# One layer of a pooling and state-space decoder: the sample states' products in one run per half, five raw buffers, exponentials and one split moved

## The chip, the cores and the metric

The kernel runs on one core of one Trainium2 chip. The metric is the device time of one execution in microseconds (us); the lower, the better. The core has several engines, each with its own in-order queue: TensorE (PE, matmuls; its weight loads are shown as PEld), VectorE (DVE), ScalarE (ACT), GpSimd (POOL) and SyncE (SP, which only issues transfers; ACT issues some too). Engines wait for each other by semaphores. Within an engine nothing overtakes: an instruction that waits holds up all that is queued behind it.

## The reference, cut to what matters

There are 1024 prompt rows and 64 sample rows (8 sequences of 8 steps), 1024 channels, one layer, all in fp32. Two branches, causal pooling and a state-space recurrence (SSD), are merged by gates.

```python
shift, scale, gate = split(silu(c) @ w_ada + b_ada)
h = rmsnorm(x, norm_g) * (1 + scale) + shift
u_pool, z_pool, z_ssm, xbc, dt, g = split(h @ w_in)            # 8224 columns
P = (pool_mix(u_pool) * silu(z_pool)) @ w_pool_out
S = gated_rmsnorm(ssd(silu(conv(xbc))) + D * xs, z_ssm) @ w_ssm_out
x = x + gate * ((sigmoid(g_pool) * P + sigmoid(g_ssm) * S) @ w_o)
y = rmsnorm(x, final_g)

# ssd, for each of 4 groups of 8 heads (64 wide, state 128), chunk by chunk
decay = exp(where(mask, acs_i - acs_j, -inf))
att = (C_i . B_j) * decay * dt_j
y   = att @ x  +  C @ (exp(acs) * h)                 # h: the state before the chunk
h   = h * exp(last) + B^T @ (exp(last - acs) * dt * x)
```

For the prompt a chunk has 128 rows and the state starts at zero. For the samples each of the 8 sequences has one chunk of 8 rows and a state that is read from memory (8 x 32 heads x 64 x 128) and written back updated.

## The kernel before

**Products with split operands.** A weight or activation is split into a high part (a copy on ACT, rounded to the matmul's fast fp32r type, tile names `whi`, `Y`, `R`, `S`, `G`) and a low part (the difference, mostly on POOL, `wlo`). Three products, high x high, high x low, low x high, replace one fp32 product. They are lines L609, L610 and L611 in the products with w_in and L360, L361 and L362 in those with w_pool_out and w_ssm_out. Accumulators lie in two pools of PSUM banks: `mm` (3 banks, `PA()`) and `ps` (5 banks, `PB()`).

**The stages.** The head (to about 82 us) makes the modulation (c @ w_ada, L277 among its products) and h with its high and low parts (L315, L327, L330). Then (to about 826 us) w_in is worked off in pairs of 128-column tiles; for each pair seven products of half size replace eight (`strassen`), and the sums on DVE before and after them are L555 (of raw weights) and L620 and L625 (of results). The first part of the pairs feeds convolution and pooling. The last ten "light" pairs (`LAST = 10`, about 600 to 826 us) make gates and z; their function is L721 (on ACT), their results are stored by L723 to memory as `gs` and `gp`. Beside them runs the SSD of the samples, `ssd_samples(g)`, a generator that is moved a step at a time, 18 steps for each of the 4 groups. Then (826 to about 1130 us) come 32 prompt chunks, their work between the products L360 to L362. The tail (from about 1130 us) has the last eight rows of products, `tail_unit(m)`, with row m's split of w_o, and at the end the product with w_o (L2000 to L2002), normalised and stored.

**Raw weights.** `pair_w` loads a pair's weights as two tiles of 512 KB, tag `rawA` with 3 buffers (L541, or L544 in two parts). A buffer is free when its splits and sums (L166 on ACT, L169 on POOL or DVE, L555 on DVE) have read it. The gate weights are loaded by L839 on the same queue, SP.

**The samples' state.** A group's 64 rows are done in two halves of 4 sequences. A half has four parts of two heads each. For a part, PE transposes the four loaded states (L1295, fp32), ACT copies them to SBUF (L1297, tags `hT` and `yt`, in turn), and PE multiplies C by them (L1304): four products of 32 columns, each in its own column tile of the array, out of `cz` (C padded to 32 columns), into a quarter of one bank `po`. An fp32 product is two instructions, so a part has eight. Then comes the update product (L1307) and the update of the state on DVE (L1310), and the state is stored. The products of one part stand behind the next part's transposes.

**Chunks.** A chunk's decays are loaded, `ch_far` masks them on POOL (L1193) and, for all but a group's first chunk, makes `cE`, an exponential on ACT (L1402); `ch_exps` makes eight exponentials on ACT (L1202); `ch_turn` transposes x and B on PE (L118, L1415) and copies B on ACT (L1417); `ch_weigh` weighs x on DVE and copies it on ACT (L1429); `ch_mix` multiplies on DVE (L1439); `ch_lows` makes low parts on DVE (L1444, L1445); `ch_inner` is PE's (L1214).

**What sets the order.** Up to the chunks, the order on each engine is made by a scheduler that simulates the program in time (`schedule_with_timeline_sim`), with the buffers as they come free. `behind(engine)` gives what is issued in it a place not before the engine's last issued instruction. From the chunks on, `in_line` fixes the order as written on all engines, and in the tail on PE, DVE, ACT and POOL.

Of the kernel before, what the change touches and what calls it, by code (L numbers as in the profile page):

```python
# [11 lines left out]
ALU = mybir.AluOpType  # L12
# [34 lines left out]
def tile_pool_ssd_step(  # L47
# [9 lines left out]
    def nm(s):  # L57
        uid[0] += 1
        return f"{s}_{uid[0]}"
# [36 lines left out]
    def PB():  # L96
        return psB.tile([P, 512], F32, tag="ps", name=nm("ps"))
# [104 lines left out]

    def x_square(i, eng):
        xt, n = xr[i]
        sqj = pa.tile([P, D], F32, tag="rawA", name=nm("sqj"), bufs=3)
        if eng is V:
            V.scalar_tensor_tensor(sqj[:n], xt[:n], 1.0, xt[:n], ALU.mult, ALU.mult, accum_out=ss[:n, i:i + 1])
        else:
            act(sqj[:n], xt[:n], AF.Square, accum_out=ss[:n, i:i + 1])
# [70 lines left out]
    def ada_out(part):  # L280
        a, b = PARTS[part]
        n = (b - a) * P // 2
        mr = pa.tile([P, 256], F32, tag="rawA", name=nm("mr"), bufs=3)
        act(mr[:, :n], pm[part][:, :n], AF.Copy)
        return mr

# [246 lines left out]
    def pair_w(c0, c1, pri, early):  # L533
        def run():
            with tc.high_priority(pri):
                raws = []
                for j in range(2):
                    r = pa.tile([P, 4, 2, P], F32, tag="rawA", name=nm("rawA"), bufs=3)
                    rows_ = w_in[0, j * 512:(j + 1) * 512]
                    if c1 == c0 + P:  # L540
                        load(r, rows_[:, c0:c0 + 2 * P].rearrange("(k p) (t c) -> p k t c", p=P, c=P))  # L541
                    else:
                        for t, c in enumerate((c0, c1)):
                            load(r[:, :, t], rows_[:, c:c + P].rearrange("(k p) c -> p k c", p=P))  # L544
                    raws.append(r)
            b11, b12, b21, b22 = raws[0][:, :, 0], raws[0][:, :, 1], raws[1][:, :, 0], raws[1][:, :, 1]
            w = []

            def add(x):
                with tc.high_priority(pri):  # L550
                    w.append(split(x, highs, eng=V if early else None))

            def diff(dst, x, y, op=ALU.subtract, eng=V):
                with tc.high_priority(pri):
                    eng.tensor_tensor(dst, x, y, op)  # L555
# [664 lines left out]
    def spt(shape, tag, bufs, dt=F32):  # L1220
        return sp.tile(list(shape), dt, tag=tag, name=nm(tag), bufs=bufs)

    def ssd_samples(g):
# [36 lines left out]
        for hf in range(2):  # L1260
# [22 lines left out]
            V.memset(cz, 0.0)  # L1283
            V.tensor_copy(cz[:, :, 0:8], Cf[:, 32 * hf:32 * hf + 32].rearrange("p (b i) -> p b i", i=8))
            yield
            po = None
            hts = {}
            for q in range(5):
                if q < 4:
                    j = 4 * hf + q  # L1290
                    if j + H0B - 1 < 8:
                        h0_load(j + H0B - 1)
                    pt = PB()
                    for b in range(4):
                        nc.tensor.transpose(pt[:, b * P:(b + 1) * P], h0s[j][:, b, :], ident)  # L1295
                    hts[q] = spt([P, 512], ("hT", "yt")[q % 2], 1)
                    act(hts[q], pt, AF.Copy)  # L1297
                if q > 0:
                    r = q - 1
                    h0 = h0s.pop(4 * hf + r)  # L1300
                    if po is None:
                        po = PB()
                    for b in range(4):
                        mm(po[32 * b:32 * b + 32, r * P:(r + 1) * P], cz[:, b, :], hts[r][:, b * P:(b + 1) * P],  # L1304
                           start=True, stop=True)
                    pu = PB()
                    mm(pu, xh[:96, r * P:(r + 1) * P], Bb[:96].rearrange("p b n -> p (b n)"), start=True, stop=True)  # L1307
                    for b in range(4):
                        cc_ = 32 * hf + 8 * b + 7
                        V.scalar_tensor_tensor(h0[:, b, :], h0[:, b, :], E2[:, r, cc_:cc_ + 1],  # L1310
                                               pu[:, b * P:(b + 1) * P], ALU.mult, ALU.add)
                    store_(new_ssm_s[0, 4 * hf:4 * hf + 4, 8 * g + 2 * r:8 * g + 2 * r + 2]
                           .rearrange("b h p n -> (h p) b n"), h0)
                if q < 4:
                    yield
            yo = spt([P, 512], "hT", 1)
            act(yo, po, AF.Copy)
            yield
# [277 lines left out]
    def samples_beside():  # L1596
        due[0] += 1
        if due[0] == 7 * LAST - 4:
            with behind(mybir.EngineType.SP):
                next(p_in)  # L1600
        if due[0] == 7 * LAST - 3:
            with behind(mybir.EngineType.SP):
                first_g.append(R())
                load(first_g[0], gp_d[0])
                first_ws[0] = ready(wp_d[0])()
        if due[0] == 7 * LAST - 2:
            next(p_in)
            with behind(mybir.EngineType.SP):
                ch_load(1)
                d_load(1)  # L1610
                first_ws[1] = ready(wp_d[1])()
                ch_load(2)
                d_load(2)
        if due[0] == 7 * LAST - 1:
            with behind(mybir.EngineType.Activation):
                ch_far(0)
                ch_exps(0)
        if due[0] == 7 * LAST:
            with behind(mybir.EngineType.DVE):
# [136 lines left out]
    ENGS = (mybir.EngineType.PE, mybir.EngineType.DVE, mybir.EngineType.Activation, mybir.EngineType.Pool, mybir.EngineType.SP,)  # L1756
    in_line(ENGS, True)
    z_load(0)
    ch_turn(0)
    ch_weigh(0)  # L1760
    ch_far(1)
# [136 lines left out]
    def tail_unit(m):  # L1898
        pf, run_ = S_unit(3, m, m_done)

        def run(w):
            k = m + EARLY
            if k < 8:
                wo_load(k, M((P, D)))
            if 0 < m < 6:
                r_load(m + 2)
            run_(w, 0)
            if m == 0:
                run_(w, 1)
# [12 lines left out]
            if m > 1:  # L1922
                samples[m - 2]()
        return (pf, run)
# [129 lines left out]
```

## Time and profile before

| what | value |
|---|---|
| time, median of 3 runs | 1290.96 us (1286.81 to 1292.78) |
| the profiled execution | 1292.2 us, of which span 1290.4 us |
| mean granted TensorE clock | 0.995 |
| busy: PE, DVE, ACT, POOL | 1255.1, 911.8, 718.4, 675.5 us |
| moved by DMA | 234.9 MB, 182 GB/s |

A row of a timeline gives the start in the span, the duration, the engine, the line, the operation, out<-in, the tiles' sizes, and how many alike were put together; in brackets stand the engine's idle time before it and what ended that. Matmuls overlap: a matmul starts when the one before it has been fed in, not when it has ended, so that steps from start to start are PE's pace. In a list of waits stand microseconds in total, how many there were, and the longest.

### The profile page before, as it was taken

Reading aid. Unit: us, or ns where it says so; the run is one execution under the profiler, and the core shown is the slowest. Engines: PE = TensorE matmul, PEld = TensorE weight load, DVE = VectorE, ACT = ScalarE, POOL = GpSimd, SP = SyncE. Lnnn points to the kernel's source line nnn. Section 1 sums busy time; section 2 is a strip of 40 time slices with the busy share of each in tenths; the row PEclk is TensorE's granted clock in tenths of the full one; section 3 lists DMA queues with packets and bytes.
Section 4 is the critical chain, followed back from the end, with each engine's and each line's share of the span. In section 5 each row is a group of like instructions: output and inputs, shape, how many; then the busy total and the mean of one; then the engine's idle time right before and its main releaser. Section 6 shows DMA issues by size and latency. Waiting matters only on the chain. (4 is left out here: it accounts for less than half of the span.)

```text
span 1290.4 us, 26363 instructions
## 1 busy us (share of the span) xinstructions
PE 1255.1 (97%) x9771; PEld 1176.8 (91%) x9771; DVE 911.8 (71%) x1584; ACT 718.4 (56%) x1685; POOL 675.5 (52%) x555
## 2 busy tenths in 40 slices
PE   7999999999999999999999999999999999999997
PEld 6779999989999999999889999989999999989786
DVE  4686778865979588776667665488667879767533
ACT  4665356465556655554554564686887768522211
POOL 1007658678869777564344443446465656636000
PEclk9999999999999999999999999999999999999999
DMA  9736354465456453444546555889666666575431
GB/s 329 243 116 220 117 164 160 143 198 178 142 164 219 144 184 126 152 154 121 160 134 202 168 155 157 288 289 317 221 197 184 185 215 207 161 270 181 158 105 50
DMA packets 225730, 234.90 MB, mean 182 GB/s; under 512 B 30370, under 2 KB 177010, under 8 KB 225595
## 3 DMA queue, kind: packets, MB, share of 16 engines
q1 hardware_dynamic: 155808, 159.01, 39.6%
q10 hardware_dynamic: 69794, 74.22, 16.8%
q8 instruction: 77, 1.26, 0.4%
q14 instruction: 51, 0.41, 0.1%
HBM read 158.67 MB, written 74.62 MB: 181 GB/s over the span
## 5 line engine op out<-in xcount | busy, mean ns | idle before, releaser
L169 POOL TENSOR_TENSOR wlo<-rawA,whi 128x512 fp32r<-128x512 f32 x120 | 186.8, 1561 | 186.6 <-ACT whi L166 102.0
L169 POOL TENSOR_TENSOR wlo<-raw,whi 128x512 fp32r<-128x512 f32 x92 | 149.4, 1631 | 125.1 <-ACT whi L166 120.7
L360 PE MATMUL mm<-Y,whi 128*128 128x352 f32 (+1 forms) x480 | 160.0, 333 | 2.7 <-DVE G L1890 2.5
L361 PE MATMUL mm<-Y,whi 128*128 128x352 f32 (+1 forms) x480 | 157.8, 329 | 0.4 <-DVE Y L1516 0.4
L362 PE MATMUL mm<-Y,wlo 128*128 128x352 f32 (+1 forms) x480 | 157.3, 328 | 0.0
L611 PE MATMUL mm<-Y,wlo 128*128 128x272 f32 x496 | 143.7, 290 | 4.1 <-POOL wlo L169 3.6
L609 PE MATMUL mm<-Y,whi 128*128 128x272 f32 x496 | 146.4, 295 | 0.3 <-ACT whi L166 0.2
L609 PE MATMUL ps<-Y,whi 128*128 128x272 f32 x496 | 144.4, 291 | 2.2 <-ACT o L809 1.6
L610 PE MATMUL ps<-Y,whi 128*128 128x272 f32 x496 | 143.1, 289 | 0.0
L610 PE MATMUL mm<-Y,whi 128*128 128x272 f32 x496 | 142.8, 288 | 0.0
L611 PE MATMUL ps<-Y,wlo 128*128 128x272 f32 x496 | 142.6, 288 | 0.0
L166 ACT ACTIVATE whi<-rawA 128x512 fp32r<-128x512 f32 x125 | 78.0, 626 | 97.9 <-PE ps L610 43.2
L1057 DVE SCALAR_TENSOR_TENSOR GA<-GA,cvT,GA 128x1112 f32<-128x1112 f32 x72 | 126.4, 1758 | 0.3
L166 ACT ACTIVATE whi<-raw 128x512 fp32r<-128x512 f32 x96 | 58.8, 626 | 90.7 <-DVE raw L555 39.3
L611 PEld LDWEIGHTS mm<-Y,wlo 128*128 128x128 f32 x496 | 93.4, 188 | 6.0 <-POOL wlo L169 4.9
L609 PEld LDWEIGHTS ps<-Y,whi 128*128 128x128 f32 x496 | 93.3, 188 | 3.7 <-ACT o L809 1.8
L360 PEld LDWEIGHTS mm<-Y,whi 128*128 128x128 f32 x480 | 90.6, 189 | 5.5 <-DVE G L1890 3.5
L609 PEld LDWEIGHTS mm<-Y,whi 128*128 128x128 f32 x496 | 93.3, 188 | 2.4 <-ACT whi L166 0.9
L610 PEld LDWEIGHTS mm<-Y,whi 128*128 128x128 f32 x496 | 93.4, 188 | 0.7 <-issue 0.6
L610 PEld LDWEIGHTS ps<-Y,whi 128*128 128x128 f32 x496 | 93.3, 188 | 0.3 <-issue 0.2
L611 PEld LDWEIGHTS ps<-Y,wlo 128*128 128x128 f32 x496 | 93.5, 188 | 0.2 <-issue 0.2
L361 PEld LDWEIGHTS mm<-Y,whi 128*128 128x128 f32 x480 | 90.5, 189 | 2.6 <-DVE Y L1516 0.9
(459 smaller groups left out, 3842.8 us busy)
## 6 DMA issues: line engine op xcount, KB each, us to landing
rawA<-in_w_in SPq DMA_DIRECT2D x46, 512.0 KB
dec<-acs_d SPq DMA_DIRECT2D x32, 512.0 KB
xbc<-GA ACTq DMA_DIRECT2D x24, 512.0 KB
xb<-xbc SPq DMA_DIRECT2D x32, 384.0 KB
rawA<-in_w_in SPq DMA_DIRECT2D x32, 256.0 KB
pw<-in_w_ssm_out ACTq DMA_DIRECT2D x32, 256.0 KB
ws<-ph ACTq DMA_DIRECT2D x32, 256.0 KB
ws<-pw SPq DMA_DIRECT2D x32, 256.0 KB
```

The costliest lines, as they stand in the source:

```text
L166: ins = act(hi[:, :, :ncols], raw[:, :, :ncols], AF.Copy)
L169: (eng or nc.gpsimd).tensor_tensor(lo[:, :, :ncols], raw[:, :, :ncols], hi[:, :, :ncols].bitcast(F32), ALU.subtract)
L360: mm(ps[:, :n], a, rh[k][:, o:o + n], start=(k == 0), stop=False)
L361: mm(ps[:, :n], a, rl[k][:, o:o + n], start=False, stop=False)
L362: mm(ps[:, :n], b, rh[k][:, o:o + n], start=False, stop=(k == nk - 1))
L609: mm(p, hi, ah, start=(k == 0), stop=False)
L610: mm(p, hi, al, start=False, stop=False)
L611: mm(p, lo, ah, start=False, stop=(k == 3))
L1057: V.scalar_tensor_tensor(d[:, :n], rp[:, k:k + n], cvT[:, 24 * k + mc:24 * k + mc + 1], d[:, :n], ALU.mult, ALU.add)
```

## The change

1. In `ssd_samples` the four parts' products with C are issued in one run of 32 instructions at the end of the half, the last part's first (r = 3, 0, 1, 2). Since all four copies are then alive together, they have four tags: `hT`, `yt`, `hU`, `hV`, two more tiles of 2 KB per partition. `po` is taken just before the run. The update products keep their places behind the next part's transposes; the last one stands behind the run. A half has as many steps as before.
2. Tag `rawA` has five buffers, not three, 8 KB more per partition; two other users of the tag say so too (`sqj`, `mr`).
3. `ch_far(0)` is no longer issued behind ACT's last instruction, and `ch_exps(0)` moves from the end of the light pairs to the start of the chunks.
4. In the tail, the split of w_o for row 0 is issued between row 0's first and second third of products, not after the third.

```diff
-        sqj = pa.tile([P, D], F32, tag="rawA", name=nm("sqj"), bufs=3)
+        sqj = pa.tile([P, D], F32, tag="rawA", name=nm("sqj"), bufs=5)
...
-                    r = pa.tile([P, 4, 2, P], F32, tag="rawA", name=nm("rawA"), bufs=3)
+                    r = pa.tile([P, 4, 2, P], F32, tag="rawA", name=nm("rawA"), bufs=5)
...
-            po = None
             hts = {}
-            for q in range(5):
-                if q < 4:
...
-                    hts[q] = spt([P, 512], ("hT", "yt")[q % 2], 1)
-                    act(hts[q], pt, AF.Copy)
+
+            def update(r):
+                h0 = h0s.pop(4 * hf + r)
+                pu = PB()
+                mm(pu, xh[:96, r * P:(r + 1) * P], Bb[:96].rearrange("p b n -> p (b n)"), start=True, stop=True)
...
+            for q in range(4):
+                j = 4 * hf + q
+                if j + H0B - 1 < 8:
+                    h0_load(j + H0B - 1)
+                pt = PB()
+                for b in range(4):
+                    nc.tensor.transpose(pt[:, b * P:(b + 1) * P], h0s[j][:, b, :], ident)
+                hts[q] = spt([P, 512], ("hT", "yt", "hU", "hV")[q], 1)
+                act(hts[q], pt, AF.Copy)
                 if q > 0:
-                    r = q - 1
-                    h0 = h0s.pop(4 * hf + r)
-                    if po is None:
-                        po = PB()
-                    for b in range(4):
-                        mm(po[32 * b:32 * b + 32, r * P:(r + 1) * P], cz[:, b, :], hts[r][:, b * P:(b + 1) * P],
-                           start=True, stop=True)
...
+                    update(q - 1)
+                yield
+            po = PB()
+            for r in (3, 0, 1, 2):
+                for b in range(4):
+                    mm(po[32 * b:32 * b + 32, r * P:(r + 1) * P], cz[:, b, :], hts[r][:, b * P:(b + 1) * P],
+                       start=True, stop=True)
+            update(3)
             yo = spt([P, 512], "hT", 1)
...
         if due[0] == 7 * LAST - 1:
-            with behind(mybir.EngineType.Activation):
-                ch_far(0)
-                ch_exps(0)
+            ch_far(0)
...
     z_load(0)
+    with behind(mybir.EngineType.Activation):
+        ch_exps(0)
     ch_turn(0)
...
             run_(w, 0)
             if m == 0:
+                wo_split(k, w4[0][:, m, :D], w4[1][:, m, :D])
                 run_(w, 1)
                 run_(w, 2)
...
-            if m < 4:
+            if 0 < m < 4:
                 wo_split(k, w4[0][:, m, :D], w4[1][:, m, :D])
-            elif k < 8 and m < 6:
+            elif m and k < 8 and m < 6:
                 wo_split(k, M((P, D), F32R), M((P, D), F32R))
```

On PE, before, in the first half of the samples' first group (row 4344 and on): a part's transposes, the products of the part before it with C, its update product, among weight products.

```order
L609 MATMUL mm_8551<-Y_484,whi_8104 128x272
L610 MATMUL mm_8551<-Y_485,whi_8104 128x272
L1295 MATMUL ps_8378<-ident,h_1359_8175 128x128 x4
L1304 MATMUL ps_8324<-yt_8322,cz_8267 32x128 x4
L1307 MATMUL ps_8389<-dec_8265,dec_8259 128x512
L611 MATMUL mm_8551<-Y_484,wlo_8105 128x272
```

On PE, now, at the end of that half (row 4369 and on); a change of line numbers comes with the diff, the products with C are L1313 now, the update products L1291 and the transposes L1304.

```order
L610 MATMUL ps_8418<-G_757,whi_8033 128x272
L611 MATMUL ps_8418<-G_756,wlo_8034 128x272
L1313 MATMUL ps_8452<-hV_8394,cz_8267 32x128 x4
L1313 MATMUL ps_8452<-hT_8277,cz_8267 32x128 x4
L1313 MATMUL ps_8452<-yt_8322,cz_8267 32x128 x4
L1313 MATMUL ps_8452<-hU_8378,cz_8267 32x128 x4
L1291 MATMUL ps_8469<-dec_8265,dec_8259 128x512
L609 MATMUL ps_8493<-Y_484,whi_8037 128x272
```

The four sets with C, which stood in four places, each between other kinds of products, now follow each other directly, 24 rows behind the last part's transposes.

On ACT, before, at the passage from the light pairs to the chunks (row 1165 and on; an ACT_TABLE_LOAD stands where the next function needs another table):

```order
L721 ACTIVATE u_1851_10958<-u_1851_10958 128x272 x2
L723 DMA gs_147<-u_1851_10958 128x544
L1202 ACT_TABLE_LOAD
L1202 ACTIVATE dec_10994<-dec_10994,acT 128x128 x8
L721 ACT_TABLE_LOAD
L721 ACTIVATE u_1850_10957<-u_1850_10957 128x272 x2
L723 DMA gs_148<-u_1850_10957 128x544
L1417 ACTIVATE bt_11239<-ps_11232 128x128
L1429 ACTIVATE xw_11245<-ps_11231 128x512
L1402 ACT_TABLE_LOAD
L1402 ACTIVATE cE_11248<-dec_11134 128x1024
```

And now (row 1168 and on):

```order
L721 ACTIVATE u_1851_10958<-u_1851_10958 128x272 x2
L723 DMA gs_147<-u_1851_10958 128x544
L721 ACTIVATE u_1850_10957<-u_1850_10957 128x272 x2
L723 DMA gs_148<-u_1850_10957 128x544
L1202 ACT_TABLE_LOAD
L1202 ACTIVATE dec_10994<-dec_10994,acT 128x128 x8
L1417 ACTIVATE bt_11239<-ps_11232 128x128
L1429 ACTIVATE xw_11245<-ps_11231 128x512
L1402 ACTIVATE cE_11248<-dec_11134 128x1024
```

The pair's last function moved ahead of the exponentials, and two of three table loads are gone.

On DVE, before, in the first half of the samples' second group, near 660 us (row 791 and on; L1251 and L1259 to L1280 are the samples' own, the rest sums of pairs):

```order
L625 TENSOR_TENSOR u_1429_8548<-u_1429_8548,ps_8898 128x272
L1251 TENSOR_TENSOR dec_8851<-dec_8851,ps_8874 64x8x64
L620 TENSOR_TENSOR u_1492_8928<-s_1491_8927,mm_9000 128x272
L1259 TENSOR_TENSOR xd_8914<-ps_8959,xd_8914 128x4x64
L620 TENSOR_TENSOR u_1493_8929<-u_1492_8928,mm_9049 128x272
L1270 TENSOR_TENSOR xw_8978<-ps_8971,wd_7450 96x512
L1278 TENSOR_TENSOR bt_8983<-ps_8976,bt_8983 32x128
```

And now:

```order
L625 TENSOR_TENSOR u_1429_8548<-u_1429_8548,ps_8898 128x272
L1251 TENSOR_TENSOR dec_8851<-dec_8851,ps_8874 64x8x64
L1259 TENSOR_TENSOR xd_8914<-ps_8959,xd_8914 128x4x64
L1270 TENSOR_TENSOR xw_8978<-ps_8971,wd_7450 96x512
L620 TENSOR_TENSOR u_1492_8928<-s_1491_8927,mm_9000 128x272
L1278 TENSOR_TENSOR bt_8983<-ps_8976,bt_8983 32x128
L620 TENSOR_TENSOR u_1493_8929<-u_1492_8928,mm_9044 128x272
```

The two samples' sums moved ahead of the pair's first L620. Elsewhere the scheduler moved rows too: on SP, the second pair's raw weight loads stand ahead of the second half of the gate weights' loads; on DVE two sums L555 of that pair moved from row 149 to rows 79 and 83, among the head's last sums for h; on PE the rows 438 to 545 (the second pair's products) are in another order, and the rows from 546 to 4315 stand as before. In the tail, POOL's first L1730 (L1728 now) stands ahead of L1886, not behind it.

More of the change, by code (lines that the diff above doesn't have):

```diff
@@ L282, in ada_out @@
         n = (b - a) * P // 2
-        mr = pa.tile([P, 256], F32, tag="rawA", name=nm("mr"), bufs=3)
+        mr = pa.tile([P, 256], F32, tag="rawA", name=nm("mr"), bufs=5)
         act(mr[:, :n], pm[part][:, :n], AF.Copy)
@@ L1285, in ssd_samples @@
             yield
-            po = None
             hts = {}
-            for q in range(5):
-                if q < 4:
[L1290 to L1293, printed above, removed]
-                    for b in range(4):
-                        nc.tensor.transpose(pt[:, b * P:(b + 1) * P], h0s[j][:, b, :], ident)
-                    hts[q] = spt([P, 512], ("hT", "yt")[q % 2], 1)
-                    act(hts[q], pt, AF.Copy)
-                if q > 0:
-                    r = q - 1
-                    h0 = h0s.pop(4 * hf + r)
-                    if po is None:
-                        po = PB()
-                    for b in range(4):
-                        mm(po[32 * b:32 * b + 32, r * P:(r + 1) * P], cz[:, b, :], hts[r][:, b * P:(b + 1) * P],
-                           start=True, stop=True)
[L1306 to L1315, printed above, removed]
@@ new lines, in update @@
+            def update(r):
[3 more added lines that the diff above has]
+                for b in range(4):
+                    cc_ = 32 * hf + 8 * b + 7
+                    V.scalar_tensor_tensor(h0[:, b, :], h0[:, b, :], E2[:, r, cc_:cc_ + 1],
+                                           pu[:, b * P:(b + 1) * P], ALU.mult, ALU.add)
+                store_(new_ssm_s[0, 4 * hf:4 * hf + 4, 8 * g + 2 * r:8 * g + 2 * r + 2]
+                       .rearrange("b h p n -> (h p) b n"), h0)
@@ L1316, in ssd_samples @@
+            for r in (3, 0, 1, 2):
+                for b in range(4):
+                    mm(po[32 * b:32 * b + 32, r * P:(r + 1) * P], cz[:, b, :], hts[r][:, b * P:(b + 1) * P],
+                       start=True, stop=True)
+            update(3)
             yo = spt([P, 512], "hT", 1)
```

## The prediction

> **What bounds the kernel now.** I read the page's busy times first, then its slices, then the list of what TensorE (PE) waited for.
>
> ```profile
> PE 1255.1 (97%) x9771; PEld 1176.8 (91%) x9771; DVE 911.8 (71%) x1584; ACT 718.4 (56%) x1685; POOL 675.5 (52%) x555
> PE   7999999999999999999999999999999999999997
> ```
>
> PE works 1255.1 of 1290.4 us; no other engine passes 71%. Only the first and the last slice are below 9. So two things can shorten the span: fewer PE microseconds, or fewer PE waits, 35.3 us in all. An engine beside PE matters only where PE waits for it.
>
> ```profile
> PE mm L611 <- POOL wlo L169: 4.7, 8, 1.1
> PE mm L360 <- DVE G L1890: 2.5, 1, 2.5
> PE ps L1295 <- DVE xd L1259: 2.4, 1, 2.4
> PE ps L118 <- DVE btl L1444: 2.1, 1, 2.1
> PE ps L1214 <- DVE dec L1439: 0.6, 1, 0.6
> ```
>
> (us in total, times, longest.) These are the waits that the change can reach. The windows give the stretches between head and tail:
>
> ```profile
> 82.00:600.00 518.00, 510.38 (x3997) 500.35 (x3997) 399.06 (x622) 288.06 (x670) 365.83 (x233) 1.00 0.49 158
> 600.00:826.00 226.00, 221.54 (x1897) 205.39 (x1896) 139.97 (x333) 115.15 (x248) 98.59 (x78) 0.99 0.58 175
> ```
>
> First number after the window: its length, then PE busy. PE is idle 7.6 and 4.5 us there, 12.1 us in 744.
>
> **Column-tiled products, one run of four sets instead of four runs.** The instructions stay the same; only their neighbours change. One set of before, among weight products:
>
> ```profile
> 628.13 0.29 PE L611 MATMUL mm<-Y,wlo 128*128 128x272 f32 x1
> 628.35 0.42 PE L1304 MATMUL ps<-yt,cz 128*32 128x128 f32 x8
> 628.70 0.39 PE L609 MATMUL ps<-Y,whi 128*128 128x272 f32 x1
> 628.93 0.29 PE L610 MATMUL ps<-Y,whi 128*128 128x272 f32 x1
> 629.06 0.29 PE L611 MATMUL ps<-Y,wlo 128*128 128x272 f32 x1
> ```
>
> Starts are what counts, since ends overlap. Undisturbed, a weight product starts 0.13 after the one before it (628.93 to 629.06). From 628.13 to 628.93 there are 0.80 us, with two such steps in it (0.25), so the set costs 0.55: 0.35 from its own start to the next product's, about 0.09 more than usual to get in and about 0.10 more on the first product behind it. With 4 groups, 2 halves and 4 sets that is 32 × 0.55 = 17.6 us. What a longer run costs is shown by the head, where the same shape stands in runs of two lengths, and a copy of a transposed state on ACT:
>
> ```profile
> 26.80 1.52 PE L277 MATMUL ps<-Y,scT 128*32 128x128 f32 x48
> 29.47 0.64 PE L277 MATMUL ps<-Y,scT 128*32 128x128 f32 x16
> 663.67 0.60 ACT L1297 ACTIVATE hT<-ps 128x512 f32<-128x512 f32 x1 [0.16 <-PE ps L1295]
> ```
>
> 32 more instructions take 0.88 us: eight of them, one set, are two rounds of four column tiles, and a further round costs 0.88/8 = 0.11. A run of four sets has eight rounds, six more than one set: 0.55 + 6 × 0.11 = 1.21 us. Eight runs: 9.7 us. Gain 8.0. Lower end: if sets don't close up, each keeps its 0.35, a run is 0.55 + 3 × 0.35 = 1.60, and the gain 4.8. Upper end: if the 0.10 on leaving a run falls away too, 8.8. I take 8.0, since L277's rows have the very shape. What covers the wait for the fourth copy: in each of the eight halves 23 or more PE rows stand between the last state's transposes and the run, 23 × 0.13 = 3 us, against the copy's 0.60. If ACT is over 2 us behind, PE waits there. The last update product and its store come later by a run, 1.2 us, and nobody in the same half waits for them.
>
> **The first exponentials, moved on ACT.**
>
> ```profile
> 826.95 0.44 DVE L625 TENSOR_TENSOR u<-u,ps 128x272 f32<-128x272 f32 x1 [1.07 <-PE ps L611]
> 827.64 1.28 ACT L1202 ACT_TABLE_LOAD   x1 [1.24 <-DMA xb<-xbc]
> 828.93 2.45 ACT L1202 ACTIVATE dec<-dec,acT 128x128 f32<-128x128 f32 x8
> 831.40 1.28 ACT L721 ACT_TABLE_LOAD   x1
> 832.69 0.75 ACT L721 ACTIVATE u<-u 128x272 f32<-128x272 f32 x2
> 833.90 0.28 ACT L1417 ACTIVATE bt<-ps 128x128 fp32r<-128x128 f32 x1 [0.46 <-ACT u L721]
> 834.69 1.28 ACT L1402 ACT_TABLE_LOAD   x1
> 835.98 1.06 ACT L1402 ACTIVATE cE<-dec 128x1024 f32<-128x1024 f32 x1
> 837.11 1.09 POOL L1193 TENSOR_SCALAR_AFFINE_SELECT dec<-dec 128x1024 f32<-128x1024 f32 x1 [12.79 <-ACT cE L1402]
> 834.27 1.22 DVE L1439 TENSOR_TENSOR dec<-dec,ps 128x1024 f32<-128x1024 f32 x1 [3.16 <-issue]
> 841.27 1.22 DVE L1439 TENSOR_TENSOR dec<-dec,ps 128x1024 f32<-128x1024 f32 x1 [2.46 <-ACT ps L1419]
> 835.54 1.09 PE L1214 MATMUL ps<-dec,xd 128*64 128x128 f32 x16 [0.56 <-DVE dec L1439]
> 843.97 0.25 PE L118 MATMUL ps<-identR,xb 128*128 128x128 f32 x1 [2.13 <-DVE btl L1444]
> ```
>
> ACT loads a table three times in seven microseconds, since the last gate function (L721) stands between two groups of exponentials. Now L721 comes first, and the exponentials and cE (L1402) share one load: two loads of 1.28 go. In the new order L721's pair can start when DVE's L625 has summed its operand, 826.95 + 0.44 = 827.4, and ends at 828.15; load and exponentials (1.28 + 2.45) end at 831.9, 2.0 before the 833.90 at which chunk 0's L1417 started. From there to cE were 0.79 and a load; without the load cE ends at 831.9 + 0.8 + 1.06 = 833.8 instead of 837.0. POOL's L1193, next exponentials and L1417 of chunk 1 follow, 3.2 earlier. DVE's first L1439, which waited for the ACT copies, comes 2.0 earlier, more than the 0.56 that PE waited; the second some 3.2 earlier, more than 2.13. Both waits go: 2.7 us, lower end 0.6 (only the first one). Late next is ACT's own pace, a chunk's exponentials and copies, of which L118's wait is the next to return: PE reaches it 0.6 earlier, DVE 3.2 earlier, and 3.2 − 2.1 − 0.6 leaves 0.5 to spare.
>
> ```profile
> 667.50:670.90 3.40, 3.01 (x19) 2.58 (x19) 3.27 (x8) 1.63 (x3) 0.86 (x1) 0.51 0.01 2
> 845.00:848.40 3.40, 3.40 (x20) 3.02 (x20) 3.40 (x8) 2.89 (x10) 2.62 (x4) 0.50 1.08 354
> ```
>
> Behind the 2.13 us wait the granted clock (third from the end) is 0.50 for 3.4 us, and 0.51 behind the 2.4 us wait at 665: half of 3.4 is 1.7 us of work lost each time. I let it go with its wait: another 1.7 (0 to 1.7). Together 4.4.
>
> The Trainium skill, "TensorE: Matmul & The Clock Gate", section "Why this matters for your kernels", warns of PE gaps above about 3 us only, and Part 1 has the clock drop after an idle window of some 3.4 us that runs freely. The trace differs: its gaps are 2.1 and 2.4 us. By that rule the slow stretches would hang on windows and not on these waits, and might stay: 3.4 us less gain (a rival below).
>
> **Five raw weight buffers.** Two buffers more, so SP issues a pair's loads earlier, and the scheduler, which plans with the buffers, puts splits and sums elsewhere: PE rows differ from row 438 to 545 and again in the samples' part.
>
> ```profile
> SPq L541 <- POOL wlo L169: 207.4, 37, 15.6
> 539.19 0.69 DVE L555 TENSOR_TENSOR raw<-rawA,rawA 128x512 f32<-128x512 f32 x1 [6.74 <-DMA rawA<-in_w_in]
> 80.01 0.72 DVE L503 TENSOR_TENSOR Y<-tf,Y 128x544 fp32r<-128x544 f32 x1 [1.52 <-ACT Y L510]
> ```
>
> SP waits 207 us for those buffers, but PE waits for the splits (L611, first list) only 4.7. That is the upper end of the gain; the lower end is a loss, below. I take 1.0, nearer to nothing, since even where DVE stood 6.74 us for a load (539.19) none of PE's eight split waits was over 1.1. In the head two L555 sums (0.69 each) now stand in DVE's queue among the sums of h (L327, L315), before 80 us: 1.4 us, which the idle 1.52 at 80.01 swallows if the loads have landed. If not, DVE stands there and PE waits for h: by the row at 539.19, 6.74 − 1.5 = 5.2 us lost. Loads cost no more bytes; two of them pass gate loads on SP's queue.
>
> The same new plan moves L1259 and L1270 ahead of one L620 on DVE:
>
> ```profile
> 667.07 0.44 DVE L620 TENSOR_TENSOR u<-s,mm 128x272 f32<-128x272 f32 x1 [6.15 <-DMA gp<-u]
> 667.42 0.42 DVE L1259 TENSOR_TENSOR xd<-ps,xd 128x256 f32<-128x256 f32 x1
> 667.89 1.11 PE L1295 MATMUL ps<-ident,h 128*128 128x128 f32 x4 [2.39 <-DVE xd L1259]
> ```
>
> L620 waits 6.15 us for a store to leave its buffer; L1259 behind it holds a PSUM bank that PE's transposes want. With L1259 in front, DVE does it before it stops at L620. PE's 2.4 goes, and the slow clock behind it (1.7): 4.1, lower end 0 if PE then stops at what else L620 holds, its accumulator. I take 4.1.
>
> **Row 0's split of w_o.**
>
> ```profile
> 1147.02 4.76 POOL L1730 TENSOR_TENSOR Y<-m,Y 128x1024 fp32r<-128x1024 f32 x2
> 1149.45 3.42 DVE L1866 TENSOR_TENSOR m<-G,m 128x1024 fp32r<-128x1024 f32 x1
> ```
>
> Two POOL subtractions, 2.4 each, run beside DVE's L1866, which takes 3.42; behind it stands L1890, for which PE waits 2.5 (first list). One subtraction now goes ahead of L1886 into POOL's idle time; the other still meets L1866, as it waits for ACT's half of row 1. Gain between 0 and 2.5; I take 0.5.
>
> **New waits.** A plan in another order has waits of its own. Upper end: as much as the 12.1 us of idle in the two windows above; lower end 0. I take a quarter, 3.0, since most rows there keep their place.
>
> **Sum.** 8.0 + 4.4 + 1.0 + 4.1 + 0.5 − 3.0 = 15.0. The profiled execution took 1292.2 us, 1.2 over the median of the three runs (1290.96); 1292.2 − 15.0 = 1277.2. I give 1277.
>
> **Rivals.**
> 1. Only the run pays. The plan's order gives new waits where it takes old ones, and ACT's chain stays late, waiting for a load (the 1.24 before 827.64). For it: PE idles under 2% between head and tail, so little can be won from waits. Against it: ACT's two loads are seen to go in the new order. 1292.2 − 8.0, and up to 1 us for the first wait at 835: about 1284.
> 2. The slow stretches stay, elsewhere (the rule above): 15.0 − 3.4 = 11.6, about 1280.5. For it: two cases are few to tie a gap to the clock. Against: both stretches stand right behind such a gap, and in the window of 744 us quoted above the clock is 0.99 to 1.00.
> 3. No change that counts: run 4.8, new waits of 3 to 5 eat it: 1288 to 1292. This needs the sets not to close up, against L277's rows.
> 4. Slower: PE waits in each half for the fourth copy (hV), which stands in ACT's queue behind other work. Eight waits of w us; the sum's 15 us are gone at w = 1.9, and past 2 us each would bring 1.7 of slow clock, so w = 2.5 gives 1292.2 − 15 + 8 × 4.2 = 1311. For it: ACT is in order and 115 of 226 us busy there. Against: 3 us of products stand in between, and a copy takes 0.6.
> 5. More: the tail's 2.5 goes as well and new waits stay under 1: about 1272.
>
> **Chances.** Forecast (1274 to 1279) 0.35; rival 2 (1279 to 1282.5) 0.20; rival 1 (1282.5 to 1286) 0.20; rival 5 (under 1274) 0.12; rival 3 0.08; rival 4 0.05. A measurement of this kernel tells about 0.5% from no change, 6.5 us: faster means under 1284.5. The forecast, rivals 2 and 5 and most of rival 1 lie there: 0.35 + 0.20 + 0.12 + 0.13 = 0.80. Within 0.5%: 0.07 of rival 1 and rival 3, 0.15. Slower 0.05. The range leaves out the far end of rival 5, the upper half of rival 3 and rival 4: 1270 to 1286.
>
> **What would show it.** Right: L1313 in eight runs of 32 instructions, about 1.0 us from the first start to the next product's; no ACT_TABLE_LOAD between the L721 near 828 and cE; no PE wait of 2 us near 665 and 843, and 1.00 in the clock there; PE busy near 1243 (8.0 and the slow stretches' 3.4 less). Wrong: a wait of PE for hV, a longer list of PE waits between 82 and 600 us, or DVE standing at its new L555 in the head for a raw weight load, where every microsecond beyond the 1.5 of idle at 80 would be lost.

## The result and the profile after

The changed kernel takes 1273.35 us (median of 6 runs, 1270.23 to 1277.6), the kernel before 1289.32 on the same chip (6 runs, 1286.6 to 1292.78): a ratio of 0.9878, 95% interval 0.9864 to 0.9891, or 16.0 us between the medians. Forecast were 1277 (1270 to 1286) and, against the profiled execution of before, 15.0 us. The profiled execution after takes 1271.29 us with a span of 1269.5, 20.9 less than the span before; so this pair of profiles shows about 5 us more than the medians do, and the runs below were partly made to find out what comes and goes with the execution.

The page after, busy times and PE's slices:

```profile
PE 1242.3 (98%) x9771; PEld 1173.9 (92%) x9771; DVE 900.9 (71%) x1584; ACT 718.0 (57%) x1683; POOL 683.1 (54%) x555
PE   7999999999999999999999999999999999999997
```

PE has the same 9771 instructions and 12.8 us less to do. Two table loads are gone from ACT (1683 instructions for 1685). PE's waits after (us in total, times, longest):

```profile
PE mm L609 <- ACT whi L166: 2.2, 3, 1.1
PE mm L611 <- POOL wlo L169: 2.0, 1, 2.0
PE ps L118 <- DVE btl L1444: 1.4, 1, 1.4
PE mm L609 <- DVE u L620: 1.2, 1, 1.2
PE ps L1291 <- DVE dec L1275: 1.0, 2, 0.6
```

The waits of 2.5 before L360 and of 2.4 before the transposes are gone, the one before L118 fell from 2.1 to 1.4, and three kinds of wait are new or grown. The run of four sets, at the end of the first half:

```profile
616.00 0.29 PE L611 MATMUL ps<-G,wlo 128*128 128x272 f32 x1
616.22 0.42 PE L1313 MATMUL ps<-hV,cz 128*32 128x128 f32 x8
616.46 0.40 PE L1313 MATMUL ps<-hT,cz 128*32 128x128 f32 x8
616.68 0.40 PE L1313 MATMUL ps<-yt,cz 128*32 128x128 f32 x8
616.90 0.40 PE L1313 MATMUL ps<-hU,cz 128*32 128x128 f32 x8
617.23 0.50 PE L1291 MATMUL ps<-dec,dec 96*128 96x512 f32 x1
617.57 0.29 PE L609 MATMUL ps<-Y,whi 128*128 128x272 f32 x1
```

From 616.22 to 617.23 the run takes 1.01 us; a set behind another costs 0.22, two rounds of 0.11, as L277's rows had it. The way in costs 0.22 for 0.13 as before, and the last set needs 0.33 up to L1291, 0.11 more than the others.

Where the time went is best seen by stages. PE's weight products are the same in every kernel, so the starts of the same products (by their count, the first, 600th, 1650th, 3300th, 3900th and last product of the pairs; the 120th and 1000th of those with w_pool_out and w_ssm_out; the last matmul) cut each trace into the same stages, the columns of the table in order. This table is worked out from the traces of all kernels that were run; in "passage", "tail" and others an s marks a stretch of slow clock in that stage.

```
kernel           head  to 160  160-300  300-515  515-590  samples  passage  chunks    tail
before         81.80s   77.60   143.25   215.25    85.19  223.55s  35.45s   230.04  191.58
before again   80.04    78.55   140.53   215.25    85.98  223.91s  35.48s   230.04  191.58
run alone      80.11    78.53   141.53   215.25    85.09  216.94s  33.52    230.04  192.59s
buffers alone  80.09    77.95   138.80   215.25    80.92  224.45s  37.03s   230.04  192.60s
exps alone     79.50    78.56   141.08   215.25    85.13  222.79s  31.92    230.00  193.17s
split alone    79.46    78.44   139.50   215.25    86.39  221.72   35.20s   230.04  190.29
changed        79.64    77.53   138.23   215.25    80.93  218.30s  32.56    230.04  190.29
changed again  79.41    77.44   138.51   215.25    80.90  216.29   32.74    230.00  191.83s
no run         79.14    77.72   138.44   215.25    80.90  224.81s  33.18    230.00  190.24
no buffers     79.86    78.57   142.82   215.25    85.35  215.10   32.11    230.00  190.24
no exps        81.29s   78.04   138.51   215.25    80.91  215.01   38.66s   230.04  190.27
run as 0,1,2,3 81.30s   78.00   138.22   215.25    80.91  218.73s  33.11    230.00  191.79s
four buffers   81.58s   78.03   140.97   215.36    80.89  215.99   34.84s   230.04  190.29
six buffers    81.22s   78.03   139.01   215.25    80.91  219.44s  31.19    230.04  190.25
```

### The profile page after: what moved, and what is told of

Read it like the earlier page. It is cut to its first block, busy times and chain, and to the rows that moved or that the text cites. A ratio compares the mean times of both kernels' runs of the same rounds, so it can differ in the third digit from the quotient of the medians.

```text
span 1269.5 us, 26341 instructions
## 1 busy us (share of the span) xinstructions
PE 1242.3 (98%) x9771; PEld 1173.9 (92%) x9771; DVE 900.9 (71%) x1584; ACT 718.0 (57%) x1683; POOL 683.1 (54%) x555
## 5 line engine op out<-in xcount | busy, mean ns | idle before, releaser
L169 POOL TENSOR_TENSOR wlo<-rawA,whi 128x512 fp32r<-128x512 f32 x120 | 189.0, 1580 | 170.5 <-ACT whi L166 95.8
L169 POOL TENSOR_TENSOR wlo<-raw,whi 128x512 fp32r<-128x512 f32 x92 | 155.1, 1693 | 122.2 <-ACT whi L166 119.3
L360 PE MATMUL mm<-Y,whi 128*128 128x352 f32 (+1 forms) x480 | 159.8, 333 | 0.7
L609 PE MATMUL mm<-Y,whi 128*128 128x272 f32 x496 | 146.3, 295 | 2.2 <-ACT whi L166 2.2
L611 PE MATMUL mm<-Y,wlo 128*128 128x272 f32 x496 | 143.5, 290 | 2.5 <-POOL wlo L169 2.0
L609 PE MATMUL ps<-Y,whi 128*128 128x272 f32 x496 | 143.8, 290 | 0.0
L611 PE MATMUL ps<-Y,wlo 128*128 128x272 f32 x496 | 142.5, 287 | 0.0
L609 PEld LDWEIGHTS mm<-Y,whi 128*128 128x128 f32 x496 | 93.5, 189 | 4.2 <-ACT whi L166 2.8
L611 PEld LDWEIGHTS mm<-Y,wlo 128*128 128x128 f32 x496 | 93.5, 189 | 2.9 <-POOL wlo L169 2.2
L360 PEld LDWEIGHTS mm<-Y,whi 128*128 128x128 f32 x480 | 90.3, 188 | 4.2 <-DVE G L1890 2.4
L609 PEld LDWEIGHTS ps<-Y,whi 128*128 128x128 f32 x496 | 93.3, 188 | 0.2
L611 PEld LDWEIGHTS ps<-Y,wlo 128*128 128x128 f32 x496 | 93.4, 188 | 0.0
```

The lines of the kernel that those rows point to most:

```text
L169: (eng or nc.gpsimd).tensor_tensor(lo[:, :, :ncols], raw[:, :, :ncols], hi[:, :, :ncols].bitcast(F32), ALU.subtract)
L360: mm(ps[:, :n], a, rh[k][:, o:o + n], start=(k == 0), stop=False)
L609: mm(p, hi, ah, start=(k == 0), stop=False)
L611: mm(p, lo, ah, start=False, stop=(k == 3))
```

## The experiments

Where a kernel changes one part, the rest is as in the kernel it is made from; none leaves work out.

**The run alone, the buffers alone, the exponentials alone, the split alone.** Each is the kernel before with one numbered part of the change, so its diff is that part's.

> The kernel before with the run of four sets alone (buffers, exponentials and the split of w_o as before). If a longer run saves what the sum said, 0.55 us becomes 0.22 to 0.24 for three of four sets: 8.0 us less PE time, median near 1281 against 1289, and each run of L1313 about 1.0 us from its first start to the next product. If the places that the scheduler gives to the rest of the samples' work cost as much again (the rival: new waits), the PE time is still 8 less, but the span falls by less than 5 and waits of PE between 600 and 826 us grow by the difference.

> The kernel before with five raw weight buffers alone. In the two traces PE lost 5.0 us less between 195 and 300 us and 4.3 less between 515 and 590 us, in places where the order on PE is the same row by row. First theory: the buffers did that (loads issued earlier, splits never late): median 7 to 10 us under the kernel before, and those waits for the splits (L611 for L169) are gone here too. Rival, the predicted 1.0: such waits come and go from one execution to the next, and the median falls by 0 to 2 us.

> The kernel before with the exponentials moved alone. Predicted 4.4 (2.7 of waits, 1.7 of slow clock); the changed kernel's trace shows 2.9 for this place, since 1.4 of the wait before L118 stays. If the slow clock hangs on the wait, 2.9 to 4.4 less; if it moves elsewhere, 1.0 to 1.5 less. Two table loads fewer on ACT in either case.

> The kernel before with row 0's split of w_o moved alone. Predicted 0.5; the changed kernel's trace shows the 2.5 us wait before L360 gone and 1.3 left of that at the end. So 0.5 to 1.5 less, which the median can hardly show; the rows show whether DVE's L1866 takes 1.2 instead of 3.4 us.

Against 1288.95 us (29 runs of before on that chip):

| kernel | median, runs | ratio, 95% interval |
|---|---|---|
| run alone | 1284.0, 8 | 0.9956 (0.9942 to 0.9969) |
| buffers alone | 1286.43, 10 | 0.9979 (0.9967 to 0.9991) |
| exponentials alone | 1287.86, 10 | 0.9981 (0.9967 to 0.9994) |
| split alone | 1287.22, 10 | 0.9983 (0.9966 to 1.0) |

*The run*: 5.0 us for 8.0 of PE time saved (its page has PE busy for 1245.4 us, 9.7 less than before; 1.7 of that goes with one slow stretch less). In the column "samples" the six executions without the run need 221.7 to 224.8 us and the eight with it 215.0 to 219.4, 6.6 less between the means. The wait near 665 us is gone, and another stands some 30 us earlier:

```profile
PE ps L1291 <- DVE dec L1275: 3.2, 3, 2.6
PE mm L611 <- POOL wlo L169: 1.1, 1, 1.1
```

These are PE's waits between 590 and 828 us in the run alone. The update product waits for the low part of the samples' inputs; the row shows the place.

```profile
638.09 0.50 PE L1291 MATMUL ps<-dec,dec 96*128 96x512 f32 x1 [2.59 <-DVE dec L1275]
```

Behind it the clock is slow for 3.4 us. So the rival of new waits was half right: 8.0 and the old wait were saved, and 5.0 remained.

*The buffers*: the first theory is right about the stages and wrong about the time. From 515 to 590 us every kernel with four buffers or more needs 80.9 and every one with three 85.1 to 86.4, 4.6 more between the means; from 160 to 300 us the kernels with three need 139.5 to 143.3, with five 138.2 to 138.8. Windows of before, cut at round times that cover most of the two stages, and of after, cut at the stages' ends, show PE's idle time vanish (length, PE busy):

```profile
160.00:300.00 140.00, 136.30 (x1059) 132.75 (x1058) 108.60 (x169) 78.72 (x191) 103.33 (x62) 1.00 0.53 172
515.00:590.00 75.00, 72.13 (x563) 70.17 (x562) 57.89 (x95) 37.37 (x82) 45.03 (x40) 1.00 0.43 144
```

```profile
157.20:295.40 138.20, 138.20 (x1085) 135.75 (x1084) 110.80 (x172) 80.13 (x194) 107.71 (x65) 1.00 0.56 179
510.65:591.60 80.95, 80.95 (x642) 79.36 (x641) 65.06 (x104) 41.37 (x84) 51.36 (x44) 1.00 0.42 135
```

PE waits for nothing at all there after the change. Of this, the median of the buffers alone shows 2.5, and its profile names a part of what is missing. The passage takes 1.6 more than before, though both have one slow stretch in it: ACT's copy L1429 waits for the store of the last gate result, which it doesn't in the kernel before, and PE waits 1.5 for L1429.

```profile
824.10 0.33 ACTq L723 DMA_DIRECT2D gs<-u  x1
824.47 0.28 ACT L1417 ACTIVATE bt<-ps 128x128 fp32r<-128x128 f32 x1 [0.40 <-ACT u L721]
828.03 0.60 ACT L1429 ACTIVATE xw<-ps 128x512 fp32r<-128x512 f32 x1 [3.28 <-DMA gs<-u]
```

The samples take about 1 more, and a slow stretch in the tail takes 1.0. The rest of the difference I can't place from one profile.

*The exponentials*: the passage takes 31.9 for 35.4. Without its slow stretch (1.7) that is 1.8 at least; the median shows 1.1, the ratio 2.4. ACT's L1429 waits for no store there (only L1417 does, 0.48), and the wait before L118 falls to 0.7.

*The split*: the tail takes 1.3 less, with the same 190.2 to 190.3 in each kernel that has the move and no slow stretch. DVE's L1866 and POOL's second subtraction, after:

```profile
1129.58 1.22 DVE L1866 TENSOR_TENSOR m<-G,m 128x1024 fp32r<-128x1024 f32 x1
1129.71 3.35 POOL L1728 TENSOR_TENSOR Y<-m,Y 128x1024 fp32r<-128x1024 f32 x1 [2.27 <-DMA whi<-ws]
```

**Taking parts out of the changed kernel, and two sizes.** "No run", "no buffers" and "no exps" are the changed kernel with that part as before. The order of the run and the number of buffers:

```diff
-            for r in (3, 0, 1, 2):
+            for r in (0, 1, 2, 3):
```

```diff
-                    r = pa.tile([P, 4, 2, P], F32, tag="rawA", name=nm("rawA"), bufs=5)
+                    r = pa.tile([P, 4, 2, P], F32, tag="rawA", name=nm("rawA"), bufs=4)
```

(and `bufs=6` in another kernel; the tag's two other users likewise)

> The changed kernel without the run of four sets: each set stands behind the next part's transposes again. Its order on DVE has the pair's L620 ahead of L1259 again, though the buffers are five, so the wait of 2.4 to 2.6 us before L1295 near 660 us should be back: then the run, not the buffers, took that wait away, against the prediction, which put it to the buffers' new plan. Time: 8.0 of PE time and that wait with its slow clock, against new waits of the run's order: 6 to 10 us above the changed kernel, 1279 to 1283. If the run's new waits ate all but 5 as in the run alone, 1278.

> The changed kernel with three raw weight buffers. If the buffers are worth the 4.2 us that the stretch from 515 to 590 us shows in each kernel with five, and nothing elsewhere, 4 us above the changed kernel, 1277 to 1278, and the waits of PE before L611, L609 and L1109 between 515 and 565 us are back. If they are worth only what they gave alone, 2.5: 1276. If the run needs them too, over 6: 1280.

> The changed kernel, but the run takes the parts as 0, 1, 2, 3 instead of 3, 0, 1, 2. The run itself should cost the same 1.0 us (the fourth copy is ready 3 us ahead in either case). But the order on DVE then has L620 ahead of L1259 again: if that order is the cause of the wait near 660 us, it is back with 2.4 to 2.6 us and a slow stretch behind it, and the kernel is 2 to 4 us over the changed one, 1275 to 1278. If that wait has another cause, no difference above 1 us.

> The changed kernel with four raw weight buffers. SP then issues each load one buffer later than with five. If the gain between 515 and 590 us needs one load more in flight, four do it: within 1 us of the changed kernel. If it needs both, 2 to 4 us above it, 1275 to 1277, and part of the waits before L611 in that stretch is back.

> The changed kernel with six raw weight buffers. Four gave 1275.4, five 1273.4. If loads still come late with five, 1 to 2 us less again, 1271 to 1272; if five are enough, no difference within 1 us.

> The changed kernel with the first exponentials where they were. The passage to the chunks takes 33 to 33.5 us without a slow stretch and 31 to 32.5 in the kernels with the move, 34 to 37 with a slow stretch. If the move is worth its clean difference, 1.3, the median is 1274 to 1276; if the slow stretch comes more often without it, up to 1277. With the 4.4 that was forecast, 1277.8.

| kernel | median, runs | ratio to before, 95% interval |
|---|---|---|
| changed | 1273.35, 6 | 0.9878 (0.9864 to 0.9891) |
| no run | 1279.74, 4 | 0.9919 (0.9902 to 0.9936) |
| no buffers | 1279.74, 4 | 0.9928 (0.9902 to 0.9954) |
| no exps | 1280.67, 7 | 0.9934 (0.9914 to 0.9955) |
| run as 0, 1, 2, 3 | 1276.42, 4 | 0.9891 (0.9868 to 0.9914) |
| four buffers | 1275.42, 4 | 0.9890 (0.9867 to 0.9912) |
| six buffers | 1271.94, 4 | 0.9870 (0.9847 to 0.9894) |

Without the run the wait of before is back, though the buffers are five:

```profile
PE ps L1295 <- DVE xd L1259: 2.6, 1, 2.6
```

That is the one wait between 640 and 670 us. With the run in the order 0, 1, 2, 3, DVE's order there is that of before again (L620 ahead of L1259), and so is the wait, somewhat shorter:

```profile
PE ps L1304 <- DVE xd L1259: 1.6, 1, 1.6
```

So DVE's order makes this wait, and the run in the order 3, 0, 1, 2, not the buffers, gave the order that hasn't it. On the whole that order is worth at most a little: 1276.42 against 1273.35, with intervals that overlap.

Without the buffers the 4.4 from 515 to 590 us are back, and 4.6 of the 160 to 300; the median is 6.4 higher, nearer the "over 6" of the expectation than to the 2.5 of the buffers alone. Four buffers have the gain of 515 to 590 in full and two waits that five hadn't in this one execution (160 to 300, passage; the second stands behind a wait of DVE's L1426 for a gate store, 4.87); six are 1.4 below five, less than the runs can tell. Six buffers are thus no proven better kernel; all three sizes lie within each other's intervals.

Without the exponentials' move the changed kernel loses 7.3, not 1.3 and not the 4.4 of the forecast: the passage takes 38.66, 6.1 more. Two windows of slow clock in a row, 6.83 us from 827.4 on, are some 3.4 of that; waits are the rest. The profile names what the move saves there: the last gate result is now stored late, and ACT's copy L1429, whose tile comes to lie where that result lay, waits for the store.

```profile
814.63 0.33 ACTq L723 DMA_DIRECT2D gs<-u  x1
815.00 0.28 ACT L1417 ACTIVATE bt<-ps 128x128 fp32r<-128x128 f32 x1 [0.40 <-PE mm L362]
818.65 0.60 ACT L1429 ACTIVATE xw<-ps 128x512 fp32r<-128x512 f32 x1 [3.37 <-DMA gs<-u]
```

The wait for the store is read from the row; that the tile's place in memory is the link is my reading of it. PE then waits 3.5 us:

```profile
PE ps L118 <- DVE btl L1444: 3.5, 1, 3.5
```

The buffers bring this wait. In the six executions with three buffers, "exps alone" and "no buffers" among them, L1429 follows L1417 at once. In the six with five it comes 1.75 to 3.37 us late (four of the rows name the store, two an instruction of DVE that ended last): 3.28 in "buffers alone" (above), 3.37 here, and 1.8 to 2.1 with the exponentials moved, where the store goes out ahead of them, as in "changed again":

```profile
815.54 0.60 ACT L1429 ACTIVATE xw<-ps 128x512 fp32r<-128x512 f32 x1 [1.75 <-DMA gs<-u]
```

With six buffers, in one execution, it doesn't wait. So the two parts help each other: between the means, slow stretches included, the move makes the passage 2.9 us shorter with three buffers and 4.9 with five.

**The kernel before and the changed kernel once more,** with nothing edited.

> The kernel before once more, to see what comes and goes with the execution. If the slow clock follows from idle time inside a window of a fixed grid (below), its stretches lie at other places than 56.5, 667.5 and 845.0 us, but each right behind a window of 3.413 us in which PE stood idle for more than about 1.7, and no such window is without one. The waits near 665 us (2.5) and before L360 in the tail (2.5) are there again. The stretch from 160 to 300 us, where two kernels with the same order gave 3.7 us of difference, lies between 139.5 and 143.3 us; the one from 515 to 590 stays at 85 to 86.

> The changed kernel once more. If five buffers make the splits sure to be in time, the stretch from 160 to 300 us is 138.2 to 138.8 again and that from 515 to 590 80.9; the samples' part keeps within 2 us of 218.3, and the passage to the chunks is 32 to 35, 1.7 of it by the clock. If the profiled execution was lucky rather than usual, these grow by some 2 us.

The second executions took 1289.84 and 1270.85 us. The two slow stretches of the kernel before follow windows with over 2.0 us of idle, as expected; in the passage of the changed kernel neither execution has one, against the expectation. Stages that vary with the execution are the head (81.8 and 80.0 for the kernel before), 160 to 300 with three buffers (143.3 and 140.5), the samples' part (218.3 and 216.3 for the changed kernel) and whatever a slow stretch falls into; the others repeat to 1 us, most to 0.1. Before's first profile lies 2.9 above the median of 1289.32, with the head's slow stretch (1.8 against the second) and the longest 160 to 300 of all (2.7 more); the changed kernel's lies 2.1 below its median. That is the 5 us by which the pair of profiles overstates the medians.

## Why the prediction was right, and where not

The time fell inside the range, 3.7 us below the forecast, and 16.0 us stand against 15.0. But terms of the sum were off in both directions, so that the total is nearer than its parts.

**The run, 8.0.** Right as PE time: 0.11 a round, 1.01 us a run, the fourth copy never waited for. What the run's own rows give is to be had in full only where nothing else comes late: alone it brought 5.0, as part of the whole 6.4.

**The exponentials, 4.4.** The order came as said, and the two loads are gone. The step that failed is "Both waits go ... leaves 0.5 to spare": 1.4 of the wait before L118 stayed. The rows after:

```profile
811.72 1.28 ACT L1202 ACT_TABLE_LOAD   x1 [0.56 <-DMA dec<-acs_d]
813.01 2.45 ACT L1202 ACTIVATE dec<-dec,acT 128x128 f32<-128x128 f32 x8
815.37 0.26 ACT L1417 ACTIVATE bt<-ps 128x128 fp32r<-128x128 f32 x1
817.42 0.60 ACT L1429 ACTIVATE xw<-ps 128x512 fp32r<-128x512 f32 x1 [1.79 <-DVE dec L1439]
814.86 0.69 DVE L1426 TENSOR_TENSOR xd<-ps,dtT 128x512 f32<-128x512 f32 x1 [1.81 <-DMA gs<-s]
```

L1417 came as early as worked out, but L1429 stood 1.79 us behind it. The row puts that down to DVE's L1439, which ended at the same time; L1429 reads what L1427 wrote, and that was ready at 816.27. In "changed again" DVE's L1426 waited only 0.47 for its store, L1439 ended 0.4 before L1429 began, and L1429 came 1.75 late all the same, by its row for the store of the last gate result. So it is this store that the sum left out: I had followed ACT's queue alone and taken L1429 to be ready, and the buffers of the same change had put a store in its way. 1.79 late with 0.5 to spare leaves 1.3, near the 1.4 that stayed; in "exps alone", without that store, 0.7 stayed. By the passage means, 35.9 us without the move and 32.7 with it, the term was 3.2.

**The buffers, 1.0.** The term that was sized worst. I took the waits of L611 for L169 (4.7 in all) as the upper end and stayed near nothing, since the longest was 1.1. But other waits went with them in every kernel with four buffers or more: L609 behind a copy on ACT (L809), and L1109. I read them as other faces of a late load. By stages the buffers took away 3.0 and 4.6, 7.6 us between the means, all of PE's idle time from 160 to 590. What they cost in the passage, by the means 0.9 us with the move and 2.9 without it, stood nowhere in the sum. Of the loss that I feared in the head, DVE standing at its new L555, nothing came: the sums run at 60.79 and 62.38 without a wait.

**The wait near 665, 4.1.** The wait went, but the attribution failed: it was the run that moved L1259, as "no run" and "0, 1, 2, 3" show (and "run alone", where L1259 stands ahead of L620 with three buffers). And its lower end came partly true. DVE still stands at L620, and PE at the accumulator that L620 holds:

```profile
658.03 0.44 DVE L620 TENSOR_TENSOR u<-s,mm 128x272 f32<-128x272 f32 x1 [4.15 <-DMA gp<-u]
658.52 0.40 PE L609 MATMUL mm<-G,whi 128*128 128x272 f32 x1 [1.24 <-DVE u L620]
```

The slow stretch only changed its place, to 604, behind a new wait of 2.0 for a split: what rival 2 said, for this one. In the second execution of the changed kernel the same wait was 1.6 and no slow stretch followed.

**The split, 0.5.** 1.3. The collision is still there, but DVE's L1866 now starts 0.13 us ahead of POOL and takes 1.22 instead of 3.42, while POOL takes 3.35 instead of 2.4. PE's 2.5 us go, and four steps of 0.47 us in place of 0.16 before L360, 7.3 us apart, give 1.2 back (their idle time, 0.14 each, is too short for the list). The Trainium skill, "SBUF — State Buffer", section "SBUF: two separate sides", has the two engines share one pair of ports, and whichever starts first holds it for its whole instruction; the two profiles show either order, with the loser 2.2 or 1.0 us longer.

**New waits, 3.0.** In the list after, L609 for ACT's copies has 1.6 more than before, L609 for L620 0.5, L1291 0.8, and the one wait for a split near 601 us is 2.0 for 1.1: 3.8, with a slow stretch behind the last one. The term was near.

Set against the stage means, the sum had 9.1 us for the samples' part (8.0 + 4.1 − 3.0), and 6.6 came, as the new waits were 0.8 longer and the slow stretch stayed; it had 4.4 for the passage, and 3.2 came; 0.5 for the tail, and 1.7 came (with its slow stretches); 1.0 for the buffers, and 7.6 came. That the total lies so near is luck in part. The chances held: rival 3 and rival 4 didn't come, and no run waited for hV.

What stays open: the stage means add to 6.6 + 7.6 + 3.2 + 1.7 = 19.1 us, the medians to 16.0. Parts alone add to 10.3, parts taken out (without the split) to 20.1. That the parts help each other is shown, and one link of it: the store in the way of L1429, which the buffers bring and the moved exponentials shorten. Why L1429 must wait for it with five buffers and not with three is not shown (that its tile comes to lie elsewhere is argued), nor what else holds back the buffers alone.

## What to carry to other kernels

Sum a part's waits over the whole stage that it can reach and not over the one kind of wait that names it: with PE full but for 12 us, the two buffers more took away several kinds of wait, and PE's idle share by windows had the right size. In an in-order engine, an instruction moved by a planner belongs to the part that moved it only when the order of that part alone has been looked at. And follow a moved instruction's operands on the other engines too, and the stores that may have to leave its tile's place: its queue is only half of what it waits for.

## What the runs showed of the hardware

The slow clock follows a rule that the kernel before shows already. Its slow stretches start at 56.5, 667.5 and 845.0 us; the distances are 179.0 and 52.0 times 3.4133 us, the length of one stretch. So there is a fixed grid of windows. I cut all 14 traces by their own grids and summed PE's idle time (gaps of over 0.2 us between a matmul's modelled end and the next start) in each window between 30 and 1200 us:

| idle in a window of 3.413 us | windows | next window at half the clock |
|---|---|---|
| below 0.90 | some 4700 | 3 |
| 0.90 to 1.64 | 70 | 2 |
| 1.64 to 1.85 | 9 | 5 |
| over 1.85 | 16 | 16 |

So a window with over 1.85 us of idle, a little more than half of it, always made the next one slow. Between 1.64 and 1.85 the idle time alone doesn't decide: the five that did so are all in the head, at 1.66 to 1.67, and the four that didn't have 1.68 to 1.80. Of the two below, one (1.14) is itself a slow window, in "no exps". The three with no idle time are all in the tail ("exps alone", "changed again", "run as 0, 1, 2, 3"), and each holds the whole of this run of products with one column:

```profile
1109.16 2.05 PE L1834 MATMUL ps<-ones,sq_acc 128*128 128x1 f32 x18
```

To the next product it takes 1.98 us. In the other 11 executions a window's edge cuts it, at most 1.91 lie in one window, and no slow stretch follows. So these products seem to count like idle time, though the profile shows PE busy; no run tests it with the run taken out.

A wait of 2.5 us makes a window slow only if enough of it falls into one window: the wait before the transposes, 2.3 to 2.6 us in each of six executions, drew a slow stretch in four of them and none in "split alone" and "no run". In "split alone" 1.80 of it fell into one window, and the clock is 1.00 around the wait and behind it:

```profile
661.50:665.50 4.00, 1.83 (x20) 1.49 (x20) 2.59 (x6) 0.91 (x2) 0.00 (x0) 1.00 0.13 50
665.50:669.00 3.50, 3.50 (x36) 3.20 (x32) 3.30 (x10) 1.18 (x4) 1.65 (x1) 1.00 0.02 5
```

The Trainium skill, "TensorE: Matmul & The Clock Gate", Part 1, has the free-running window of 3413 ns, which these traces bear out, and the slow state after an idle window; here a window idle for a little over half was enough, and the measurement decides. For a forecast from these traces: a single wait below 1.6 us cost itself alone, but in the head two, of 1.3 and 0.4, fell into one window; one of 2 to 2.6 cost up to 1.7 more, by chance of its place, and the 3.5 in "no exps" two slow windows.
